# Three modulation sums moved to the tensor engine, a fourth final operand, earlier row gathers: one joined change to a two-layer trunk kernel

## The chip, the cores and the metric

The kernel runs on 1 NeuronCore of one Trainium2 chip as a single launch. The metric is device time in microseconds of that core. All data is float32; 512 tokens of width 1024 pass through two layers. "PE" is the tensor engine, "DVE" the vector engine, "ACT" the scalar engine, "POOL" GpSimd, "SP" the sync engine, which only issues transfers here.

## The reference, cut to what matters

```python
c_act = jax.nn.silu(c)
for layer in range(2):
    mod = c_act @ ada_w[layer] + ada_b[layer]              # (1024) @ (1024, 6144), 25 MB of weights a layer
    shift1, scale1, gate1, shift2, scale2, gate2 = jnp.split(mod, 6, axis=-1)
    h = rmsnorm(x, norm1_w[layer]) * (1 + scale1) + shift1
    if layer == 0:   # one projection -> pooling channels | q | k | v, pooling mixer and chunk attention, output projection
        mix = concat(pool_mixer(u), chunk_attention(q, k, v, rel_bias)) @ mix_w_out
    else:            # Mamba-2 mixer: projection, convolution, dt = softplus(h @ w_dt + dt_bias), chunked scan, gated norm
        mix = mamba2_mixer(h, ...)
    x = x + gate1 * mix
    h2 = rmsnorm(x, norm2_w[layer]) * (1 + scale2) + shift2
    x = x + gate2 * hier_moe(h2, ...)                        # 32 experts, top 2 inside the best group
return rmsnorm(x, final_norm_w)
```

## The kernel before, in words

**Modulation.** A third of a layer's `mod` (2048 columns) is a "part": `ada(layer, part, eng)` is a generator that loads eight 1 MB tiles of `ada_w` (128 rows by 2048 columns) into a ring of five buffers (tag `w8`) and, one step at a time, adds tile k times `ccol[:, k]` to the running sum on DVE (lines 189 and 191). After the eighth step four matrix products with a 128x32 block of ones add up the 128 partitions (line 198), each product writing its own 32 partitions of one PSUM bank. `ada(0, 1)`, `ada(0, 2)` and `ada(1, 0)` run inside the attention of layer 0, their steps spread over the calls of `fill()` by the list `FILL`; `ada(1, 1)` and `ada(1, 2)` run inside the Mamba mixer. Part 0 of layer 0, which the first norm needs, has its own code: `ada_loads` and `ada_sums(b)` (lines 507 to 580), in two halves b of four column blocks of 128 each for shift and scale.

**Start of layer 0.** `x` is loaded and transposed (line 532). `ada_sums(0)`, `modulate(0)`, `v_products(0)`, then the same for half 1: v = h @ w_v, with h and the weights each split into a high part (ACT, line 110) and a low part (DVE or POOL by the table `LO`, line 111), three products per pair (lines 434 to 436). `late_loads` (line 271) loads a row of zeros and three small vectors of layer 1 (`ssm_D`, `ssm_dt_bias`, `ssm_A_log`), each spread over 128 partitions by the transfer itself. Then `Dense` streams the columns of q, k and u: it loads (line 402), splits, and multiplies (lines 426 to 429). `scores(m)` (line 655) is the first step of attention.

**The order of the work.** The program fixes what depends on what, and a planner with estimated costs sets the order on each engine; each engine then runs its own list strictly in order, so that an instruction that waits holds up all behind it. Inside `manual_schedule` blocks the order is as written. Transfers issued by SP share one queue.

**The expert stage.** `Moe.run` loops over 17 units u of 128 token slots (16 pairs of experts and one overflow unit). In iteration u the PE does the hidden layer of unit u (line 1036), then the results of unit u-1 (line 1057). The results of most units are written to `yd` in DRAM (line 1067); at the end `ygather` (line 1176) adds the rows of `yd` to `x` with eight indirect transfers of 512 KB, two for each of the four token tiles. The units 8, 10, 13, 14, 15 and 16 do not go through DRAM: their results stay in SBUF as an "operand" (`parts_y`: high part, low part, one-hot matrix) and are added to `x` by products with the one-hot matrix (`products`, line 1079) and `padd` (line 1086). Units 8, 10 and 13 get this two iterations later; 14, 15 and 16 together in `combine`, after the loop. `combine` runs a list of steps (`STEPS` in layer 0): `xn` adds tile n, `hn` is a stage of the next norm of tile n, `wn` splits a weight of the next mixer. Before `combine`, `ahead()` loads the dt weight `wdt` (1024 rows of 32 columns), and splits it on ACT and DVE (lines 1438 to 1440).

Of the kernel before, what the change touches and what calls it, by code (L numbers as in the profile page):

```python
# [20 lines left out]
P = 128  # L21
T = 512
# [14 lines left out]
GAT = 15  # L37
# [16 lines left out]
HOLD = 7  # L54
PINS = 3
# [7 lines left out]
LO = {"v": "G", "e": "VVG", "m": "V", "o": "GVV", "s": "VV"}  # L63
# [4 lines left out]
STEPS = "x0 h0 x1 h1 h0 x2 h2 h0 h1 x3 h2 h3 h3 h0 h1 h2 h1 w1 h3 w2 h3 h2"  # L68
# [7 lines left out]
def trunk_kernel(ctx, tc, x, c, ada_w, ada_b, norm1_w, norm2_w, mix_w_in, pool_w, pool_scale,  # L76
# [86 lines left out]

    def ada(layer, part, eng, first=None):
# [19 lines left out]
        load(1)  # L184
        for k in range(KD):
# [8 lines left out]
        for _ in range(SLACK):  # L194
            yield
        p = ps(name=f"pada{layer}{part}")
        for q in range(4):
            PE.matmul(p[32 * q:32 * q + 32, :], ones[:, 0:32], ws[KD - 1][:, q * 512:(q + 1) * 512], start=True,
                      stop=True, skip_group_check=True)
# [290 lines left out]
    def even_mixer(layer):  # L490
        with ExitStack() as es:
# [15 lines left out]
            def ada_loads(b):  # L507
                SP.dma_start(adb[0:64:32, b * 512:(b + 1) * 512], dap(ada_b, b * 512, [[D, 2], [1, 512]]))
                for k in range(0, KD, 2):
# [3 lines left out]
                    aw[b, k], aw[b, k + 1] = (t[:, d].rearrange("p q n -> p (q n)") for d in range(2))  # L513
# [27 lines left out]
            def modulate(b):  # L541
# [12 lines left out]
            def v_products(b):  # L554
                for kk in (4 * b, 4 * b + 2):
# [8 lines left out]
            def ada_sums(b):  # L564
                V.tensor_scalar(aw[b, 0], aw[b, 0], ccol[:, 0:1], None, op0=ALU.mult)
                for k in range(1, KD):
                    V.scalar_tensor_tensor(aw[b, k], aw[b, k], ccol[:, k:k + 1], aw[b, k - 1], op0=ALU.mult,
                                           op1=ALU.add)
                p = ps(name=f"pada00{b}")
                for q in range(2):  # L570
                    PE.matmul(p[32 * q:32 * q + 32, :], ones[:, 0:32], aw[b, KD - 1][:, q * 512:(q + 1) * 512],
                              start=True, stop=True, skip_group_check=True)
                m = adb[0:64, b * 512:(b + 1) * 512]
                V.tensor_add(m, p[0:64], m)
                p = ps((P, 4, 64), name=f"pm00{b}")
                for q in range(4):
                    PE.transpose(p[:, q, :], m[:, q * P:(q + 1) * P], ident[0:64, 0:64])
                ks = slice(4 * b, 4 * b + 4)
                V.scalar_tensor_tensor(ab[:, 0, 0, ks], p[:, :, 32], 1.0, n1w[0][:, ks], op0=ALU.add, op1=ALU.mult)
                V.tensor_copy(ab[:, 0, 1, ks], p[:, :, 0])  # L580
# [3 lines left out]
            late_loads()  # L584
# [5 lines left out]
            v_products(1)  # L590
# [117 lines left out]
            adas = [ada(0, 1, V), ada(0, 2, V), ada(1, 0, V)]  # L708
# [81 lines left out]
    class Moe:  # L790
# [282 lines left out]
        def products(self, i, parts):  # L1073

            ps2 = [ps(name=f"pyc{self.layer}{i}{hf}") for hf in range(2)]
            for hf, p in enumerate(ps2):
                for n, part in enumerate(parts):
                    for q in range(2):
                        PE.matmul(p, part[2][:, i * P:(i + 1) * P], part[hf][:, q * 512:(q + 1) * 512],  # L1079
                                  start=n + q == 0, stop=n == len(parts) - 1 and q == 1)  # L1080
            return ps2
# [6 lines left out]
        def run(self, before_end=None):  # L1088
# [30 lines left out]
            def results(u, between=None):  # L1119
# [3 lines left out]
                             self.parts_y[max(u - NPAIR + 2, 0)] if last(u) else None)  # L1123

            ts = {}
            for u in range(NPAIR + 1):
# [20 lines left out]
                if 1 < u < NPAIR and last(u - 2):  # L1147
                    for i in range(NT):
                        self.padd(i, self.products(i, self.parts_y[:1]))
# [8 lines left out]
                if u == GAT:  # L1158
                    self.ygather()
                    for n in range(2):  # L1160
                        t = we([P, 2, 2 * T], F32R, f"yl{n}_{layer}")
                        o = we([P, 2, 2 * T], F32R, f"yo_{layer}")[:, 0, 0:T] if n else ot[:, T:2 * T]
                        self.parts_y.append((t[:, 0], t[:, 1], o))
                if u == 1:
# [256 lines left out]
    def odd_mixer(layer, prev):  # L1421
        with ExitStack() as es:
# [382 lines left out]
```

## Time and profile before

| what | value |
|---|---|
| median of three runs | 1119.99 us (1119.96 to 1123.87) |
| profiled execution: its own time, and its span | 1120.03 us, 1118.3 us |
| PE busy | 973.2 us, 87% of the span |
| DVE busy | 800.3 us, 72% |
| ACT, POOL busy | 388.9 us, 300.2 us |
| mean granted PE clock | 0.932 of full speed |
| moved by DMA | 263.88 MB, 236 GB/s |

The profile is of one execution. A matmul's duration overlaps that of the next, so the distance between the starts is its price where they follow without a gap. The granted clock has two levels, 1.2 and 2.4 GHz; a mean between 0.5 and 1.0 is a mixture. The stages in the trace: 0 to 86 us start of layer 0 (norm, v, first q and k), to 221 attention and pooling, to 262 output projection, to 301 router, to 435 experts, to 470 norm and dt of layer 1, to 862 Mamba mixer, to 930 its output projection, to 985 router, to about 1097 experts, then the last sums and the final norm.

### The profile page before, as it was taken

The numbers are of one execution on the slowest core, as the hardware profiler recorded it, in microseconds if no ns is written. First come the engines' busy times: TensorE is split into PE (matmuls) and PEld (weight loads), VectorE is DVE, ScalarE is ACT, GpSimd is POOL, SyncE is SP. The second block draws the span as 40 slices with busy tenths as digits, with TensorE's granted clock in tenths as the row PEclk, the third lists the DMA queues.
The fourth block names the chain that finished last, engine by engine and source line by source line (L and its number), as shares of the span: only waits on it lengthen the run. The fifth ranks groups of instructions, "written<-read, shape, count | busy, mean of one in ns | idle before, by whom it ended". The sixth has DMA issues, their size and how long they took to land. (4 is left out here: it accounts for less than half of the span.)

```text
span 1118.3 us, 15578 instructions
## 1 busy us (share of the span) xinstructions
PE 973.2 (87%) x5474; PEld 729.5 (65%) x5474; DVE 800.3 (72%) x1650; ACT 388.9 (35%) x753; POOL 300.2 (27%) x329
## 2 busy tenths in 40 slices
PE   4588788699699996898999899899989999799994
PEld 3466466388556654776786777777766878556653
DVE  6717986654565874789997989887797555564976
ACT  3135332425123232433444333443433325222332
POOL 4413100204231122411513416244142004231124
PEclk9789888799799998899999999999999999799997
DMA  9476876598699979536473465554334945699987
GB/s 332 139 265 168 286 282 252 215 364 330 209 364 414 411 229 255 210 107 198 143 264 88 135 194 159 190 158 113 126 109 152 333 154 209 204 390 415 412 278 185
DMA packets 140200, 263.88 MB, mean 236 GB/s; under 512 B 19917, under 2 KB 82337, under 8 KB 134994
## 3 DMA queue, kind: packets, MB, share of 16 engines
q1 hardware_dynamic: 129122, 235.40, 60.1%
q0 software_dynamic: 8928, 20.97, 7.2%
q10 hardware_dynamic: 2064, 6.42, 1.4%
q8 instruction: 47, 0.77, 0.3%
q14 instruction: 39, 0.32, 0.1%
HBM read 254.19 MB, written 20.11 MB: 245 GB/s over the span
## 5 line engine op out<-in xcount | busy, mean ns | idle before, releaser
L1036 PE MATMUL ph<-w,xT 128*64 128x256 f32 (+1 forms) x1152 | 132.1, 374 | 0.9 <-DVE xT L1020 0.7
L1036 PEld LDWEIGHTS ph<-w,xT 128*64 128x64 f32 x1152 | 86.8, 139 | 51.8 <-issue 10.9
L189 DVE SCALAR_TENSOR_TENSOR ada<-ada,ccol,ada 128x2048 f32<-128x2048 f32 x35 | 87.1, 2489 | 0.2
L1003 POOL DMA_INDIRECT xg<-xnd,toks x32 | 32.3, 1008 | 149.8 <-PE pxt L1015 122.6
L1057 PE MATMUL pyy<-w,hidT 128*64 128x512 f32 x272 | 65.9, 605 | 4.2 <-ACT hidT L1049 4.2
L1038 ACT ACTIVATE th<-ph 128x128 f32<-128x128 f32 x34 | 9.4, 278 | 160.8 <-PE pht L1047 137.1
L1022 ACT ACTIVATE xT<-pxt,mc 128x128 f32<-128x128 f32 x136 | 51.3, 458 | 17.9 <-PE pxt L1015 10.9
L1062 DVE SCALAR_TENSOR_TENSOR y<-pyy,wsl,gate 128x512 f32<-128x512 f32 x68 | 48.1, 744 | 6.1 <-DMA yd<-y 4.5
L1015 PE MATMUL pxt<-ident,xg 128*128 128x128 f32 x272 | 37.9, 284 | 15.5 <-DVEq L1383 7.9
L1086 DVE TENSOR_TENSOR x<-x,pyc 128x512 f32<-128x512 f32 x64 | 40.4, 682 | 14.1 <-PE pyc L1079 8.0
L1039 DVE SCALAR_TENSOR_TENSOR th<-th,ph 128x128 f32<-128x128 f32 x34 | 9.8, 287 | 55.7 <-ACT th L1038 55.7
L1020 DVE TENSOR_SCALAR xT<-pxt,mc 128x128 f32<-128x128 f32 x136 | 46.6, 405 | 1.4 <-PE pxt L1015 1.4
L1581 DVE TENSOR_SCALAR ms<-lb,acs 128x128 f32<-128x128 f32 x128 | 41.0, 359 | 5.9 <-DMA lb<-acd 3.6
L1015 PEld LDWEIGHTS pxt<-ident,xg 128*128 128x128 f32 x272 | 34.5, 194 | 16.2 <-issue 15.6
L1548 DVE SCALAR_TENSOR_TENSOR cvx<-pdx,cw,cvx 128x511 f32<-128x511 f32 (+2 forms) x48 | 35.4, 738 | 6.7 <-ACT cvx L1545 6.6
L1178 POOL DMA_INDIRECT x<-yd,row x16 | 25.1, 1571 | 50.0 <-DMA xgfw<-in_final_norm_w_dram 22.3
L1584 POOL TENSOR_TENSOR ms<-ms,cbm 128x512 f32<-128x512 f32 x16 | 32.0, 2001 | 17.8 <-ACT ms L1583 16.0
L1057 PEld LDWEIGHTS pyy<-w,hidT 128*64 128x64 f32 x272 | 16.5, 136 | 28.1 <-issue 19.4
L1079 PE MATMUL pyc<-yh,yot 128*128 128x512 f32 x128 | 33.7, 398 | 1.0 <-DVE yot L1070 1.0
L469 DVE TENSOR_TENSOR sor<-sor,gate 128x1024 f32<-128x1024 f32 x16 | 20.4, 1276 | 18.0 <-DMA sor<-in_ssm_w_out_dram 17.9
L661 ACT ACTIVATE scs<-scs,mx 128x512 f32<-128x512 f32 (+3 forms) x32 | 17.7, 555 | 36.2 <-DVE mx L660 32.8
L1079 PEld LDWEIGHTS pyc<-yh,yot 128*128 128x128 f32 x128 | 23.4, 188 | 9.6 <-issue 1.9
(1074 smaller groups left out, 2778.4 us busy)
## 6 DMA issues: line engine op xcount, KB each, us to landing
w<-in_moe_w_dram SPq DMA_DIRECT2D x192, 512.0 KB
ada<-in_ada_w_dram SPq DMA_DIRECT2D x40, 1024.0 KB
yd<-y SPq DMA_DIRECT2D x22, 512.0 KB
ada<-in_ada_w_dram SPq DMA_DIRECT2D x16, 512.0 KB
wx<-in_ssm_w_in_dram SPq DMA_DIRECT2D x16, 512.0 KB
wz<-in_ssm_w_in_dram SPq DMA_DIRECT2D x16, 512.0 KB
lb<-acd SPq DMA_DIRECT2D x32, 256.0 KB
sor<-in_ssm_w_out_dram SPq DMA_DIRECT2D x16, 512.0 KB
```

The costliest lines, as they stand in the source:

```text
L189: a = eng.scalar_tensor_tensor(ws[k], ws[k], ccol[:, k:k + 1], ws[k - 1], op0=ALU.mult, op1=ALU.add)
L1003: d = GP.indirect_dma_start(out=xg, out_offset=None, in_=xnd[:, :], in_offset=bass.IndirectOffsetOnAxis(ap=idx, axis=0), bounds_check=T - ...
L1015: PE.transpose(p[:, q, :], xv[:, 4 * hf + q, :], ident)
L1020: V.tensor_scalar(xT[:, k, :], p[:, q, :], a, b, op0=ALU.mult, op1=ALU.add)
L1022: S.activation(xT[:, k, :], p[:, q, :], AF.Identity, bias=b, scale=a)
L1036: PE.matmul(ph[64 * j:64 * j + 64, n:n + h, :], xT[:, k, 64 * j:64 * j + 64], w13[n][:, :, k, :], start=k == 0, stop=k == KD - 1, skip_gro ...
L1057: PE.matmul(py[64 * j:64 * j + 64], hT[:, 64 * j:64 * j + 64], w2[:, s], start=True, stop=True, skip_group_check=True)
L1062: V.scalar_tensor_tensor(y[:, s], py, self.wsl[:, slot:slot + 1], self.gate2[:, s], op0=ALU.mult, op1=ALU.mult)
L1079: PE.matmul(p, part[2][:, i * P:(i + 1) * P], part[hf][:, q * 512:(q + 1) * 512], start=n + q == 0, stop=n == len(parts) - 1 and q == 1)
L1086: V.tensor_add(xst["x"][i][:, s], xst["x"][i][:, s], p)
L1548: V.scalar_tensor_tensor(a[:, sh:], p[:, :T - sh], cw[:, tap, ch:ch + 1], a[:, sh:], op0=ALU.mult, op1=ALU.add)
L1581: V.tensor_scalar(ms[:, h, :], lb[:, h, :], acs[:, cq, 4 * g + h:4 * g + h + 1], 0.0, op0=ALU.subtract, op1=ALU.min)
```

## The change

The parts 0, 1 and 2 of layer 0's modulation and part 0 of layer 1 are summed on the PE: tile k is the moving operand of a product whose stationary operand is column k of `ccol`, broadcast to 32 columns, and the eight products accumulate in PSUM. `ada(..., None)` has one yield fewer. In `ada_sums` the even and odd k go to separate quarters of the bank, which are added after the transposes. The split's low parts in the v stage go to DVE alone, and `v_products` is called in finer pieces. `late_loads` loads the three vectors as one-partition rows; `head_rows` spreads them with a product with ones and three kinds of copies. In the experts, unit 13 is no longer added in iteration 15: it is a fourth operand of `combine`, whose tiles 0 and 1 are begun with three operands; `ygather` is issued at the end of iteration 14. The load of `wdt` moves to iteration 10, its split to a step `w0` of `combine`, its low part to POOL.

```diff
-GAT = 15
+GAT = 14
+EARLY = 10
-LO = {"v": "G", ...}
+LO = {"v": "V", ...}
-STEPS = "x0 h0 x1 h1 h0 x2 h2 h0 h1 x3 h2 h3 h3 h0 h1 h2 h1 w1 h3 w2 h3 h2"
+STEPS = "x0 h0 x1 h1 h0 x2 h2 h0 h1 x3 h2 h3 h3 h0 h1 h2 h1 w0 w1 h3 w2 h3 h2"
...
+    def ada_mm(p, k, w, first, last):
+        for q in range(4):
+            PE.matmul(p[32 * q:32 * q + 32, :], ccol[:, k:k + 1].to_broadcast([P, 32]), w[:, q * 512:(q + 1) * 512],
+                      start=first, stop=last, skip_group_check=True)
...
             yield
+            if not eng:
+                if not k:
+                    p = ps(name=f"pada{layer}{part}")
+                ada_mm(p, k, ws.pop(k), k == 0, k == KD - 1)
+                continue
...
     def late_loads():
         SP.dma_start(yd[len(MAIN) * P:, :], zrow)
+        hrow = st_.tile([1, 3, 32], F32, name="hrow")
+        for n, src in enumerate((ssm_D, ssm_dt_bias, ssm_A_log)):
+            SP.dma_start(hrow[:, n, :], dap(src, 0, [[0, 1], [1, 32]]))
+        return hrow
+
+    def head_rows(hrow):
+        p = ps((P, 3, 32), name="phr")
+        PE.matmul(p, ones[0:1, :], hrow, start=True, stop=True)
         for q in range(2):
-            SP.dma_start(dcol[64 * q:64 * q + 64, :], dap(ssm_D, q, [[0, 64], [2, 16]]))
-        SP.dma_start(dtb, dap(ssm_dt_bias, 0, [[0, P], [1, 32]]))
-        SP.dma_start(arow, dap(ssm_A_log, 0, [[0, P], [1, 32]]))
+            V.tensor_copy(dcol[64 * q:64 * q + 64, :], p[64 * q:64 * q + 64, 0, q::2])
+        V.tensor_copy(dtb, p[:, 1, :])
+        V.tensor_copy(arow, p[:, 2, :])
...
-                    (V if g % 2 else GP).tensor_sub(parts[1][g], xa[g], parts[0][g].bitcast(F32))
+                    V.tensor_sub(parts[1][g], xa[g], parts[0][g].bitcast(F32))
...
             def ada_sums(b):
-                V.tensor_scalar(aw[b, 0], aw[b, 0], ccol[:, 0:1], None, op0=ALU.mult)
-                for k in range(1, KD):
-                    V.scalar_tensor_tensor(aw[b, k], aw[b, k], ccol[:, k:k + 1], aw[b, k - 1], op0=ALU.mult,
-                                           op1=ALU.add)
                 p = ps(name=f"pada00{b}")
+                for k in range(0, KD, 2):
+                    for d in range(2):
+                        for q in range(2):
+                            o = 64 * d + 32 * q
+                            PE.matmul(p[o:o + 32, :], ccol[:, k + d:k + d + 1].to_broadcast([P, 32]), aw[b, k][:, d, q],
+                                      start=k == 0, stop=k == KD - 2, skip_group_check=True)
...
             modulate(1)
-            v_products(1)
+            v_products(2)
+            head_rows(hrow)
+            v_products(4, 6)
...
-            adas = [ada(0, 1, V), ada(0, 2, V), ada(1, 0, V)]
+            adas = [ada(0, 1, None), ada(0, 2, None), ada(1, 0, None)]
...
-                if 1 < u < NPAIR and last(u - 2):
+                if 1 < u < NPAIR - 1 and last(u - 2):
...
                 if u == GAT:
                     self.ygather()
-                    for n in range(2):
-                        t = we([P, 2, 2 * T], F32R, f"yl{n}_{layer}")
-                        o = we([P, 2, 2 * T], F32R, f"yo_{layer}")[:, 0, 0:T] if n else ot[:, T:2 * T]
+                    wide = [wp.tile([P, 2048], F32R, tag="w8", name=f"y{n}_{layer}", bufs=W8) for n in ("l0", "oh")]
+                    y = [wide[0].rearrange("p (h n) -> p h n", h=2)]
+                    y += [we([P, 2, 2 * T], F32R, f"yl{n}_{layer}") for n in (1, 2)]
+                    for t, o in zip(y, (ot[:, T:2 * T], wide[1][:, 0:T], wide[1][:, T:2 * T])):
                         self.parts_y.append((t[:, 0], t[:, 1], o))
...
-                p = [self.products(i, self.parts_y) for i in range(NT)]
+                p = self.products((0, 1), self.parts_y[:-1], False)
+                p = self.products((0, 1), self.parts_y[-1:], True, p)
+                p += self.products((2, 3), self.parts_y, True)
...
-                w = prev.y_tile("wdt")
-                wdt.append(w[:, 0:256].rearrange("p (k c) -> p k c", k=KD))
+            def early():
+                wdt.append(small.tile([P, KD, NLOG], F32, tag="wr", name="wdt", bufs=1)[:, :, 0:32])
                 SP.dma_start(wdt[0], w_in[:, 6144:6176].rearrange("(k p) c -> p k c", p=P))
+            def splits(n):
+                if n:
+                    return dense.split(n, GP)
                 wdt.append(ws4(F32R, "whl")[:, 0:512].rearrange("p (k c) -> p k c", k=KD))
-                split(wdt[1][:, :, 0:32], wdt[1][:, :, 32:64], wdt[0], V)
+                split(wdt[1][:, :, 0:32], wdt[1][:, :, 32:64], wdt[0], GP)
```

## Rows read from the trace of the kernel before

**Rows 1.** From the table by stage: from and to in us, its length, busy time (and instructions) of PE, PE weight loads, DVE, ACT and POOL, granted PE clock, DMA share, GB/s.

```profile
34.00:58.00 24.00, 15.35 (x56) 10.95 (x56) 13.91 (x13) 2.49 (x3) 9.50 (x4) 0.78 0.30 84
...
85.70:221.00 135.30, 108.25 (x500) 76.38 (x500) 108.71 (x222) 52.33 (x127) 23.44 (x20) 0.86 0.69 241
...
301.00:403.00 102.00, 100.92 (x762) 62.38 (x762) 66.49 (x189) 31.24 (x92) 19.61 (x19) 1.00 1.01 392
...
435.00:470.00 35.00, 22.64 (x138) 21.19 (x139) 23.94 (x50) 15.75 (x33) 15.65 (x17) 0.76 0.74 270
470.00:862.00 392.00, 361.07 (x1826) 287.50 (x1825) 337.85 (x530) 151.65 (x219) 127.46 (x90) 0.97 0.49 150
...
1082.00:1118.30 36.30, 20.41 (x104) 12.40 (x99) 24.19 (x53) 10.90 (x27) 18.40 (x17) 0.84 0.77 174
```

**Rows 2.** From the DMA queues between 36 and 60 us: mean busy share in 40 equal slices (tenths), packets and how many of them are small.

```profile
DMA  9610000000000000000011001111112677879996
...
DMA packets 5080, 1.74 MB, mean 73 GB/s; under 512 B 2434, under 2 KB 4906, under 8 KB 5069
```

**Rows 3.** From the instructions in order of time, those that issue transfers: start, duration of the issue.

```profile
30.99 3.52 SPq L274 DMA_DIRECT2D dcol<-in_ssm_D_dram  x2
...
41.09 4.32 SPq L402 DMA_DIRECT2D wq<-in_mix_w_in_dram  x1
```

**Rows 4.** From the waits between 30 and 62 us: which engine and line waited for whom, us in total, times, longest.

```profile
ACT q0h L110 <- DMA wq<-in_mix_w_in_dram: 13.0, 1, 13.0
...
PE pdq L426 <- ACT q0h L110: 7.4, 1, 7.4
...
PE accv L436 <- POOL hlo L550: 2.2, 1, 2.2
```

**Rows 5.** From the instructions in order of time on PE and ACT in the start stage: start, duration, in brackets the idle time before them.

```profile
11.60 8.78 PE L532 MATMUL pt<-dgx,x 128*128 128x128 f32 x64
25.26 1.92 PE L571 MATMUL pada<-ada,ones 128*32 128x512 f32 x4 [4.88 <-DVE ada L567]
...
37.80 0.80 PE L436 MATMUL accv<-vw0h,hlo 128*128 128x512 f32 x1 [2.16 <-POOL hlo L550]
...
42.13 0.39 PE L434 MATMUL accv<-vw0h,hhi 128*128 128x512 f32 x1
...
43.05 0.39 PE L435 MATMUL accv<-vw0l,hhi 128*128 128x512 f32 x1
...
85.73 0.70 PE L655 MATMUL sc<-kT,qT 64*128 64x512 f32 x2 [0.69 <-ACT kT L696]
...
23.13 1.06 ACT L110 ACTIVATE vw0h<-vr 128x1024 fp32r<-128x1024 f32 x1 [2.33 <-DMA vr<-in_mix_w_in_dram]
```

**Rows 6.** From the list of groups of DVE instructions between 85.7 and 221 us: count, busy time and mean ns of one, idle time before them.

```profile
L189 DVE SCALAR_TENSOR_TENSOR ada<-ada,ccol,ada 128x2048 f32<-128x2048 f32 x21 | 52.2, 2485 | 0.2
```

**Rows 7.** From the waits of PE between 85 and 222 us.

```profile
PE pada L198 <- DVE ada L189: 9.1, 1, 9.1
PE sc L655 <- DVE c L111: 6.7, 1, 6.7
PE pdu L426 <- DVE mx L658: 3.9, 2, 2.0
PE pdq L426 <- DVE mx L658: 3.4, 1, 3.4
```

**Rows 8.** From the instructions in order of time on PE: the four products with ones of `ada(0, 1)` and of `ada(0, 2)` (eight instructions each).

```profile
128.85 1.93 PE L198 MATMUL pada<-ada,ones 128*32 128x512 f32 x8
...
164.16 1.06 PE L198 MATMUL pada<-ada,ones 128*32 128x512 f32 x8
```

**Rows 9.** From the instructions in order of time from 405 to 448 us, on PE, ACT, DVE and POOL.

```profile
407.02 3.94 PE L1079 MATMUL pyc<-yh,yot 128*128 128x512 f32 x16
...
422.74 0.72 PE L1079 MATMUL pyc<-yh,yot 128*128 128x512 f32 x2
...
433.92 0.61 PE L1079 MATMUL pyc<-yl,yo 128*128 128x512 f32 x2
...
440.78 3.78 PE L350 MATMUL pt<-xh,x 128*128 128x128 f32 x16 [6.25 <-DVE xh L347]
446.87 1.38 PE L350 MATMUL pt<-xh,x 128*128 128x128 f32 x10 [2.31 <-DVE xh L347]
...
435.05 0.42 ACT L110 ACTIVATE whl<-wdt 128x256 fp32r<-128x256 f32 x1 [10.75 <-DMA wdt<-in_ssm_w_in_dram]
...
435.84 2.47 DVE L1086 TENSOR_TENSOR x<-x,pyc 128x512 f32<-128x512 f32 x4
...
409.34 1.60 POOL L1178 DMA_INDIRECT x<-yd,row  x1 [19.25 <-DVE x L1086]
```

**Rows 10.** From the DMA queues between 416 and 436 us, the line of the queue that SP issues to (packets, MB, share of 16 engines).

```profile
q1 hardware_dynamic: 1057, 0.14, 5.6%
```

**Rows 11.** From the instructions in order of time at the end: SP's write of unit 12's rows, POOL's first gather, DVE's sums for unit 13 and the first sum of the end.

```profile
1070.17 0.33 SPq L1067 DMA_DIRECT2D yd<-y  x1
...
1081.47 1.60 POOL L1178 DMA_INDIRECT x<-yd,row  x1 [22.31 <-DMA xgfw<-in_final_norm_w_dram]
...
1076.86 3.68 DVE L1086 TENSOR_TENSOR x<-x,pyc 128x512 f32<-128x512 f32 x6 [1.91 <-PE pyc L1079]
...
1098.70 1.28 DVE L1086 TENSOR_TENSOR x<-x,pyc 128x512 f32<-128x512 f32 x2 [4.06 <-DMA x<-yd,row]
```

More of the change, by code (lines that the diff above doesn't have):

```diff
@@ L184, in ada @@
         load(1)
+        p = None
         for k in range(KD):
@@ L193, in ada @@
                 tc.keep_in_program_order(a)
-        for _ in range(SLACK):
+        for _ in range(SLACK if eng else 0):
             yield
[L196 to L199, printed above, removed]
+        if eng:
+            p = ps(name=f"pada{layer}{part}")
+            for q in range(4):
+                PE.matmul(p[32 * q:32 * q + 32, :], ones[:, 0:32], ws[KD - 1][:, q * 512:(q + 1) * 512], start=True,
+                          stop=True, skip_group_check=True)
         m = b
@@ L512, in ada_loads @@
                         SP.dma_start(t[:, d], dap(ada_w, (k + d) * P * 6 * D + b * 512, [[6 * D, P], [D, 2], [1, 512]]))
-                    aw[b, k], aw[b, k + 1] = (t[:, d].rearrange("p q n -> p (q n)") for d in range(2))
+                    aw[b, k] = t
             def v_loads(b):
@@ L564, in ada_sums @@
             def ada_sums(b):
-                V.tensor_scalar(aw[b, 0], aw[b, 0], ccol[:, 0:1], None, op0=ALU.mult)
-                for k in range(1, KD):
-                    V.scalar_tensor_tensor(aw[b, k], aw[b, k], ccol[:, k:k + 1], aw[b, k - 1], op0=ALU.mult,
-                                           op1=ALU.add)
                 p = ps(name=f"pada00{b}")
[L570 to L575, printed above, removed]
+                for k in range(0, KD, 2):
[4 more added lines that the diff above has]
+                                      start=k == 0, stop=k == KD - 2, skip_group_check=True)
+                m = adb[:, b * 512:(b + 1) * 512]
+                V.tensor_add(m, p, m)
+                p = ps((P, 4, P), name=f"pm00{b}")
                 for q in range(4):
-                    PE.transpose(p[:, q, :], m[:, q * P:(q + 1) * P], ident[0:64, 0:64])
+                    PE.transpose(p[:, q, :], m[:, q * P:(q + 1) * P], ident)
                 ks = slice(4 * b, 4 * b + 4)
-                V.scalar_tensor_tensor(ab[:, 0, 0, ks], p[:, :, 32], 1.0, n1w[0][:, ks], op0=ALU.add, op1=ALU.mult)
-                V.tensor_copy(ab[:, 0, 1, ks], p[:, :, 0])
+                two = st_.tile([P, 2, 4], F32, name=f"two{b}")
+                V.tensor_copy(two, p[:, :, 0:64:32].rearrange("p q n -> p n q"))
+                V.tensor_add(two, two, p[:, :, 64:P:32].rearrange("p q n -> p n q"))
+                V.scalar_tensor_tensor(ab[:, 0, 0, ks], two[:, 1], 1.0, n1w[0][:, ks], op0=ALU.add, op1=ALU.mult)
+                V.tensor_copy(ab[:, 0, 1, ks], two[:, 0])
             ada_loads(1)
             v_loads(1)
-            late_loads()
+            hrow = late_loads()
             ada_sums(0)
@@ L1071, in results, with products @@
                                     op0=ALU.add, op1=ALU.is_equal)
[L1073 to L1081, printed above, removed]
+        def products(self, tiles, parts, stop=True, sums=None):
+            out = sums or [[ps(name=f"pyc{self.layer}{i}{hf}") for hf in range(2)] for i in tiles]
+            for i, ps2 in zip(tiles, out):
+                for hf, p in enumerate(ps2):
+                    for n, part in enumerate(parts):
+                        for q in range(2):
+                            PE.matmul(p, part[2][:, i * P:(i + 1) * P], part[hf][:, q * 512:(q + 1) * 512],
+                                      start=not sums and n + q == 0, stop=stop and n == len(parts) - 1 and q == 1,
+                                      skip_group_check=True)
+            return out
         def padd(self, i, ps2):
@@ L1086, in padd, with run @@
                 V.tensor_add(xst["x"][i][:, s], xst["x"][i][:, s], p)
-        def run(self, before_end=None):
+        def run(self, before_end=None, early=None):
             layer = self.layer
@@ L1451, in after @@
                     yield from hT_tile(layer, i, h_hi, h_lo)
-                prev.combine([after(i) for i in range(NT)], STEPS, lambda n: dense.split(n, GP))
+                prev.combine([after(i) for i in range(NT)], STEPS, splits)
                 prev.close()
```

14 lines of the change are left out of this document (8 added, 6 removed).

## The prediction

> **What bounds the kernel now.** I read the table by stage first, then the waits and the order of time inside the stages that the change touches. The table [rows 1] shows that no one engine sets the whole time. From 301 to 403 us (experts) PE is busy 100.9 of 102 us and DMA is full as well; from 470 to 862 us (Mamba mixer) DVE is busy 338 of 392 us beside PE at 361. The change leaves the work of these two almost as it is. Time is lost elsewhere: from 34 to 58 us, where PE works 15.4 of 24 us at a granted clock of 0.78 while DMA is busy 0.30 of the time; in attention (85.7 to 221 us), where PE and DVE each work 108 of 135 us and PE's clock is 0.86; from 435 to 470 us, with PE at 22.6 of 35 us and a clock of 0.76; and after 1082 us.
>
> In the first of these a small thing blocks a large one. SP issues the two loads of `dcol` at 31 us and the first weight of q at 41.1 us [rows 3]. The queue view shows DMA going from full to nearly idle soon after 36 us and staying there for some 15 us, with 2434 packets below 512 bytes [rows 2]; `dcol` by its shape is 2 x 64 x 16 single elements, 2048 of these. The weight of q stands behind them: ACT waits 13.0 us for it, with the modulation of half 1 behind that wait, and PE 7.4 us [rows 4].
>
> In attention, 23.1 of PE's 27.05 idle us end with a DVE instruction [rows 7], and 52.2 us of DVE's work are the running sums of modulation [rows 6]. At 435 us ACT has waited 10.75 us for the dt weight; DVE's first sum of `combine` follows at 435.84, and PE's first transpose of the new norm at 440.78, though PE's own products ended at 434.5 [rows 9]. At the end the first gather starts at 1081.47 and the first tile is added at 1098.70, the wait ended by that tile's gather [rows 11].
>
> **The change part by part.** Negative numbers are gains.
>
> *Start, -12.* Before, half 0's products with ones start at 25.26, and the v products run without a break from 37.80 [rows 5]: 12.5 us for those products, the row's sum, transposes, modulation and splits. After, the sums follow the transposes of x on PE, which end at 11.60 + 8.78 = 20.4; the weights are there, since the v weight queued behind them was being split at 23.13 [rows 5]. A step of one pair of k is eight instructions on four quarters, the form that took 1.06 us at the full and 1.93 us at half clock [rows 8]: four steps end at 20.4 + 4.2 = 24.6, or 28.1. The rest costs what it did, 37.8 - 25.3 - 1.9 = 10.6, less the 2.2 us for which PE waited for POOL's low part [rows 4], now DVE's: 33. Half 1's sums no longer stand on DVE among modulation and splits, for which I take one more: 32 instead of 37.8, -6. From there to the first scores before took 85.7 - 37.8 = 48 us. It holds 142 products of 0.23 us, the distance of the rows at 42.13 and 43.05 [rows 5], 32.7 us; after, 4 x 1.06 for half 1, 2 us for a slow beginning, 3 us for waits: 42, another -6. Between -4 (sums at half clock in both halves, +7, and some of the wait left) and -15 (no waits).
>
> The cover for the rest: the spreading of the three rows is one small product and four small copies on a DVE freed of sixteen sums; if it is late nobody asks for `dtb` before layer 1. What is late next is the supply of split weights, whose buffers come free only as products end.
>
> *Attention, -6.* Taken from DVE: three times seven sums, 52.2 us [rows 6], and the first steps. Added to PE: 24 steps of 1.06 = 25.4 us, less the three products with ones (1.93 and 1.06 are in the rows; 4.9 with the third at the larger): +20.5, so 128.8 us busy. PE's idle 27 us I cut to 9: the two waits for DVE's sums go (9.1 and 6.7), the others shrink but some stay, because PE still waits for the first scores to be read before it has a free bank, and one bank is now held through a whole part. The clock: a mean of 0.86 means the low level in 28% of the stage, 38 us; 11 to 30 us of these PE was busy, so 5 to 15 us were lost to it. With fewer holes I give back 9. Sum 128.8 + 9 - 9 = 129 against 135.3. Ends: 118 (idle 4, all 15 back), -17; and 144 (idle 15, none back), +8. Behind a PE step that waits for its tile stands all of PE's list, and behind SP's next tile of `ada_w`, which waits for a buffer, stand the next weights of q, k and u.
>
> Here a rule may be weighed against a row. Four products take 1.06 us [rows 8]. The Trainium skill, "FP8 and Floating Point Precision", section TensorE Precision Notes, states that true FP32 takes four passes through the array. Worked out by that page alone, as an estimate, a step of four products of 512 columns is 4 x 4 x 512 columns at 2.4 GHz, 3.4 us; 24 steps would be 82 instead of 25 us, and the whole change would come out near 1150. The row has four quarters sharing the time of one, in the form that the change uses; the sum goes by the row.
>
> *From layer 0 to layer 1, -8.* Unit 13's 16 products leave iteration 15 (3.94 us, row at 407.02) and come back at the end: 48 took 434.5 - 422.7 = 11.8 us, 0.245 each, so 3.9. PE's products end at 434.5 as before. The wait of ACT for the dt weight goes: its buffer was a result tile, now it is loaded at iteration 10. Tile 0 needs its second gather, the fifth; at the end of the kernel it was added 17.2 us after the first gather began [rows 11], which here is 409.34 + 17.2 = 426.6 [rows 9] even with no gain. So DVE's sums no longer hold PE: tile 0's transposes follow at 434.5 (440.78), at full clock 2.2 us instead of 3.78 (ten took 1.38), and tile 1's at 434.5 + 6.1 - 1.6 = 439 instead of 446.87 [rows 9]. Between -5 (slow clock, first step alone) and -10. The load's 1024 rows now fall where DMA is full: the 1057 packets of SP's queue were 5.6% of 20 us [rows 10], 1.1 us, which PE's lead hides, or not: +1. The low part on POOL is a quarter of a weight's; it stands between splits that come later anyway.
>
> *End, -1.* Gathers wait for the write of unit 12's rows, issued at 1070.17. The first gather began 3.3 us after tile 0's sums for unit 13 (1076.86, two of six in 3.68 us: 1078.1) [rows 11]. So what held it was a transfer, and without those sums it is still held; I take 1 us, 0 to 3.3. In layer 0 the sums did hold it.
>
> Sum: -12 - 6 - 8 - 1 = -27. The profiled execution took 1120.03 us (span 1118.3), as the median, 1119.99: 1093.
>
> **The rivals.** *PE takes the place of DVE:* attention gives nothing (idle 11, 2 us of clock back, 138) and the start -8: 1120 - 8 - 8 - 1 = 1103. For it: PE is already at 108 of 135 us; against: DVE's sums head the two longest waits.
>
> *More:* start -14, attention -15, transition -9, end -3: 1079. For it: every hole of PE in attention ends with DVE; against: scores, exponent and transposes form a chain of their own.
>
> *No change within 0.5%* (5.6 us, about what a measurement can tell from none): the mixer, where DVE is at 338 of 392 us, would have to wait out what comes earlier. No row shows it waiting for time.
>
> *Slower, one mechanism:* PE runs dry on `ada_w`. A tile of 1.05 MB at 392 GB/s [rows 1] takes 2.7 us, a step 1.06; with the ring empty each step waits 1.6 us, and PE, unlike DVE, has everything behind it. To lose the 27 us and 5.6 more, 33 us, 21 of 24 steps would have to find it empty: 1126 or more. Against: five buffers, and DMA at 0.69 in this stage.
>
> *Quarters one after the other:* if the four products of a step did not share their time, a step would be 4 x 1.06 = 4.2 us of PE, 24 of them 102 instead of 25 us: 1170. Against it: the 1.06 us are those of all four, in eight instructions [rows 8]. The Trainium skill's page named above, with its four passes and no sharing, gives the 1150 stated there.
>
> **How the numbers follow.** My forecast, 1093 (alone 1085 to 1101), gets 0.55; PE in DVE's place 0.22; more 0.13; no change 0.05; PE dry 0.03; quarters in a row 0.02. Faster by over 0.5% is 0.55 + 0.22 + 0.13 = 0.90, within it 0.05, slower 0.05. The range goes from just below the 1079 case to beyond 1103: 1077 to 1108; less than that leaves out too much, since start and attention each have ends some 10 us from my value.
>
> **What would show it.** Start: DMA busy around 40 us, q's weight split before 50, scores before 76. Attention: PE's idle below 15 us, clock above 0.9, DVE below 60 us; wrong if PE waits for transfers of `ada` or is busy above 135. Transition: PE's transposes directly behind `pyc`, no wait of ACT for the dt weight. End: first gather less than 2 us earlier relative to the write of unit 12. The prediction is wrong if the mixer or the experts, left alone, become longer by what the start gains, or if a step on PE takes more than 1.3 us.

## The result, and the profile after

The kernel after takes 1090.74 us (median of 4 runs, 1089.82 to 1094.89) against 1120.91 of the kernel before in the same comparison: ratio 0.9734, 95% interval 0.9702 to 0.9765. The forecast was 1093, in a range of 1077 to 1108. The profiled execution is the longest of the four, 1094.89 us with a span of 1093.0; it stands 25 us below the profiled execution of before, where the medians stand 30 apart.

The start stage first: from the table by stage, then in order of time on PE, DVE, SP and ACT.

```profile
31.80:77.10 45.30, 41.37 (x184) 30.21 (x184) 14.02 (x23) 14.78 (x18) 3.12 (x3) 0.93 0.68 230
36.00:46.00 10.00, 10.00 (x59) 5.86 (x58) 1.60 (x2) 2.12 (x2) 0.04 (x1) 0.89 0.18 67
```

```profile
22.09 3.64 PE L593 MATMUL pada<-ada,ccol 128*32 128x512 f32 x32
31.83 0.79 PE L457 MATMUL accv<-vw0h,hhi 128*128 128x512 f32 x1 [4.45 <-ACT hhi L572]
40.70 3.64 PE L593 MATMUL pada<-ada,ccol 128*32 128x512 f32 x32
45.01 1.21 DVE L112 TENSOR_TENSOR vw4l<-vr,vw4h 128x1024 fp32r<-128x1024 f32 x1
46.25 0.39 SPq L425 DMA_DIRECT2D wq<-in_mix_w_in_dram  x1
51.15 1.04 ACT L111 ACTIVATE q0h<-wq 128x1024 fp32r<-128x1024 f32 x1
75.50 1.06 ACT L111 ACTIVATE q1h<-wq 128x1024 fp32r<-128x1024 f32 x1 [2.80 <-DMA wq<-in_mix_w_in_dram]
76.46 0.58 ACT L723 ACTIVATE kT<-pdk 128x512 f32<-128x512 f32 x1
77.09 2.43 PE L682 MATMUL sc<-kT,qT 64*128 64x512 f32 x16 [2.73 <-ACT kT L723]
```

Four steps take 3.64 us, 0.91 each. The v products start at 31.83 (forecast 32) and the first scores at 77.09 instead of 85.73 [rows 5]. The issue of q's weight takes 0.39 instead of 4.32 us [rows 3], but it comes later, at 46.25, because its buffer is held by a split (`vw4l`, which ends at 46.22) that stands on DVE behind the second sum. DMA therefore still has a hole (0.18 from 36 to 46 us), of another kind: in it nothing is asked for. PE now works through it (10.0 of 10 us), which is why it costs less than the hole of before.

Attention by stage, PE's waits in it, and steps on PE:

```profile
77.10:201.10 124.00, 117.97 (x669) 73.49 (x669) 53.49 (x199) 50.90 (x125) 21.67 (x19) 1.00 0.76 270
```

```profile
PE pm L306 <- DVE adab L215: 3.1, 1, 3.1
PE sc L682 <- ACT kT L723: 2.7, 1, 2.7
PE py L664 <- DVE pl L659: 1.7, 1, 1.7
```

```profile
85.11 4.50 PE L168 MATMUL pada<-ada,ccol 128*32 128x512 f32 x40
97.15 1.06 PE L168 MATMUL pada<-ada,ccol 128*32 128x512 f32 x8
```

124 instead of 135.5 us, with PE idle for 6, its clock at 1.00, and DVE at 53.5 instead of 108.7 us. Five steps in a row take 4.50, so one is 0.9; a single one takes 1.06, as in [rows 8], and 12 of the 24 stand alone. None of PE's waits in this stage is for a tile of `ada_w`.

From layer 0 to layer 1, in order of time on PE, DVE and POOL:

```profile
388.44 1.60 POOL L1210 DMA_INDIRECT x<-yd,row  x1 [18.24 <-DVE th L1067]
399.13 0.73 PE L1107 MATMUL pyc<-yh,yot 128*128 128x512 f32 x2
406.71 1.28 DVE L1115 TENSOR_TENSOR x<-x,pyc 128x512 f32<-128x512 f32 x2 [5.29 <-PE pyc L1107]
413.77 1.95 PE L373 MATMUL pt<-xh,x 128*128 128x128 f32 x16
418.02 4.10 PE L373 MATMUL pt<-xh,x 128*128 128x128 f32 x32 [2.30 <-DVE xh L370]
427.47 0.33 PE L1512 MATMUL pdt<-sh_hi,whl 128*64 128x256 f32 x1 [1.66 <-POOL whl L112]
```

The transposes of the new norm follow the products with no idle time between (6.25 before, [rows 9]), at 1.95 instead of 3.78 us. DVE's first sum waits for PE, no longer for anything of the dt weight. A small new wait is there: the low part on POOL, which I had put at nothing, is waited for by `pdt` for 1.66 us.

The end, on SP, POOL, PE and DVE:

```profile
1044.98 0.33 SPq L1094 DMA_DIRECT2D yd<-y  x1
1055.90 1.68 POOL L1210 DMA_INDIRECT x<-yd,row  x1 [22.27 <-issue]
1062.55 0.73 PE L1107 MATMUL pyc<-yh,yot 128*128 128x512 f32 x2
1073.52 1.29 DVE L1115 TENSOR_TENSOR x<-x,pyc 128x512 f32<-128x512 f32 x2 [8.71 <-DMA x<-yd,row]
```

The first gather starts 10.9 us behind the write of unit 12's rows (11.3 before, [rows 11]), and from it to the end of the span are 37.1 us (36.8). PE and DVE are done earlier, and DVE's wait for the gather grows from 4.06 to 8.71 us.

### The profile page after: what moved, and what is told of

It reads as the page before. It is cut to its first block, busy times and chain, and to the rows that moved or that the text cites. A ratio compares the mean times of both kernels' runs of the same rounds, so it can differ in the third digit from the quotient of the medians.

```text
span 1093.0 us, 15960 instructions
## 1 busy us (share of the span) xinstructions
PE 985.5 (90%) x5700; PEld 726.6 (66%) x5700; DVE 715.6 (65%) x1607; ACT 388.7 (36%) x753; POOL 282.9 (26%) x324
## 5 line engine op out<-in xcount | busy, mean ns | idle before, releaser
L1066 DVE SCALAR_TENSOR_TENSOR th<-th,ph 128x128 f32<-128x128 f32 x34 | 9.8, 287 | 57.2 <-ACT th L1065 57.2
L1115 DVE TENSOR_TENSOR x<-x,pyc 128x512 f32<-128x512 f32 x48 | 30.4, 682 | 20.9 <-DMA x<-yd,row 11.4
L1620 DVE TENSOR_SCALAR ms<-lb,acs 128x128 f32<-128x128 f32 x128 | 37.8, 335 | 6.5 <-DMA lb<-acd 4.2
L202 DVE SCALAR_TENSOR_TENSOR ada<-ada,ccol,ada 128x2048 f32<-128x2048 f32 x14 | 34.9, 2496 | 0.1
L1670 PE MATMUL pyd<-ms,xdt 128*64 128x128 f32 x256 | 20.2, 291 | 9.5 <-DVE ms L1623 9.5
L1622 ACT ACTIVATE ms<-ms 128x512 f32<-128x512 f32 x32 | 19.8, 623 | 24.6 <-DVE ms L1620 24.5
L1637 PE MATMUL pxd<-ident,cvx 128*128 128x128 f32 x64 | 11.6, 316 | 17.2 <-DVE cvx L1591 17.2
(1079 smaller groups left out, 2770.2 us busy)
```

Of the source, the lines that this page charges most:

```text
L1115: V.tensor_add(xst["x"][i][:, s], xst["x"][i][:, s], p)
L1620: V.tensor_scalar(ms[:, h, :], lb[:, h, :], acs[:, cq, 4 * g + h:4 * g + h + 1], 0.0, op0=ALU.subtract, op1=ALU.min)
```

## The experiments

The change in parts, each put alone into the kernel before; then single costs and waits in the kernel after. The marks, in us, are read from each profile's order of time; "mixer" is from the first to the last row of `pxd`, "rest" from there to the end of the span. Each row of marks is one execution, so that a spread in them may be of kernels or of executions.

```
kernel       first    output   atten-  new norm  mixer  rest    ratio to before
             scores   proj.    tion    transp.                  (95% interval)
before        85.7    221.2    135.5    440.8    328.8  291.3
loads_only    80.1    215.6    135.4    435.1    329.2  290.8   0.9940 (0.9915-0.9965)
sums_only     81.2    211.7    130.5    432.5    332.0  291.4   0.9958 (0.9935-0.9981)
start_all     75.6    206.2    130.6    426.9    328.4  290.8   0.9900 (0.9870-0.9929)
att_only      86.4    214.2    127.8    434.1    331.3  292.8   0.9928 (0.9903-0.9952)
wdt_only      85.6    218.4    132.8    434.2    330.4  293.6   0.9947 (0.9922-0.9972)
moe_wdt       84.8    216.4    131.6    431.6    328.4  291.6   0.9938 (0.9911-0.9964)
after         77.1    201.1    124.0    413.8    331.4  291.6   0.9734 (0.9702-0.9765)
act_write     75.5    202.1    126.6    416.0    331.5  286.8   0.9711 (0.9668-0.9754)
v_third       74.7    203.5    128.8    416.4    331.0  291.6   0.9812 (0.9778-0.9847)
combo         73.5    203.6    130.2    416.7    325.4  289.3   0.9749 (0.9716-0.9782)
three_edits   73.0    194.3    121.3    410.2    332.2  287.5   0.9648 (0.9623-0.9673)
```

**The start.** Whole, its loads alone, its sums alone:

```diff
 loads_only: late_loads() and head_rows(hrow) of the kernel after; the rest as before
 sums_only:  ada_sums, v_products and LO["v"] of the kernel after; late_loads() as before
 start_all:  both
```

> The kernel before with the start stage of the kernel after, and nothing else of the change: the sums of half 0 and half 1 as products with c, the low parts on DVE, the three head rows as one short row each. Theory A (the three parts of the change add up, as the two traces suggest): first scores near 77 us instead of 85.7, all of it kept to the end, 9 us, ratio 0.992 (0.990 to 0.994). Theory B (the parts hang together: the attention stage is bound by DVE and would wait for its sums of modulation whatever the start does): first scores earlier, but 3 us or less at the end, ratio above 0.997.

> The kernel before with the short loads alone: ssm_D, ssm_dt_bias and ssm_A_log as three rows on one partition, spread by a product with ones, in place of loads of single elements and of broadcast rows. Theory A (the element loads hold up q's weight, and the sums on DVE are a second, separate cost): q's weight split before 45 us instead of 56, first scores 4 to 6 us earlier, ratio 0.995 to 0.996. Theory C (the jam is the whole gain of the start): as much as the whole start stage, 8 to 9 us, ratio 0.992. Theory D (DVE's sums are the whole gain, the weight is waited for only because DVE is late): under 1 us, ratio above 0.999.

> The kernel before with the sums of half 0 and half 1 in the start as products with c and the low parts on DVE, while dcol, dt_bias and A_log are loaded as before, element by element. With the whole start stage the first scores came at 75.6 us, with the short loads alone at 80.1, before at 85.7. Theory A (two costs one after the other): 4 to 5 us, first scores near 81 us, ratio 0.996. Theory J (the late weight of q covers what the sums give, so that they only count once it is there): q's weight split at 54 us or later as before, first scores at 84 us or later, under 2 us, ratio above 0.998.

First scores 10.1, 5.6 and 4.5 us earlier: the two costs add up at this mark, and theory A holds for all three. Its detail did not: the expectation for `loads_only` names 56 us for the split of q's weight before, where the trace has 58.99, and asks for less than 45 after. With the short loads q's weight is issued at the same time as before (41.09, [rows 3]) but split at 50.79 instead of 58.99, held at the end by a buffer and not by the transfer:

```profile
41.46 0.39 SPq L411 DMA_DIRECT2D wq<-in_mix_w_in_dram  x1
50.79 1.06 ACT L110 ACTIVATE q0h<-wq 128x1024 fp32r<-128x1024 f32 x1 [4.38 <-PE accv L444]
```

With the sums alone (ACT, in order of time) the weight is as late as before, yet the gain is there: the modulation of half 1 now stands ahead of the wait for it, so that wait has less behind it.

```profile
48.80 1.99 ACT L549 ACTIVATE hhi<-xa 128x1024 fp32r<-128x1024 f32 x2
59.41 1.06 ACT L110 ACTIVATE q0h<-wq 128x1024 fp32r<-128x1024 f32 x1 [8.62 <-DMA wq<-in_mix_w_in_dram]
```

**Attention alone**, `adas` and `ada` of the kernel after in the kernel before:

```diff
-            adas = [ada(0, 1, V), ada(0, 2, V), ada(1, 0, V)]
+            adas = [ada(0, 1, None), ada(0, 2, None), ada(1, 0, None)]
```

> The kernel before with the three parts of modulation in attention as products with c on PE, and nothing else of the change. Theory A (in attention PE and DVE waited for each other, and the work that moved costs PE 24 steps of 0.9 us): from the first scores to the first product of the output projection 124 us instead of 135.5, PE's clock at 1.00 there, ratio 0.989 to 0.991 (10 to 12 us). Theory B (PE takes DVE's place, and the stage is shorter in the kernel after only because the start left its weights loaded earlier): 132 us or more, ratio above 0.997.

```profile
86.40:214.20 127.80, 119.68 (x668) 74.62 (x669) 58.01 (x200) 52.40 (x127) 21.84 (x20) 0.99 0.75 261
```

Theory A in kind (B asked for 132 us and more), at 0.9928 less than it asked for: 8 us, not 10 to 12. The table suggests why. Kernels with DVE's sums took 130.5 to 135.5 us here with the same code in this stage, mean 132.8 of six; those with all steps on PE took 124.0 to 127.8, mean 126.1 of three. The profiles of the kernels before and after happen to be the ends of both: 11.5 us between them, 6.7 between the means.

**What a step costs where it stands**, and whether four quarters share their time:

```diff
 few_steps, in ada(): one step of eight
-                ada_mm(p, k, ws.pop(k), k == 0, k == KD - 1)
+                if not k:
+                    ada_mm(p, k, ws[k], True, True)
 one_wide, in ada_mm(): one product for the four quarters
+        PE.matmul(p, ccol[:, k:k + 1].to_broadcast([P, P]), w[:, 0:512], start=first, stop=last, ...)
```

> The kernel after, with one step of products per part of modulation in attention instead of eight: 21 of 24 steps are left out, and with them seven eighths of those three sums; the weights are still loaded. It prices the steps where they stand. Theory A (the stage is bound by PE, and the steps cost what they take): 21 x 0.9 = 19 us less, 105 us from the first scores to the output projection. Theory F (the steps fill holes that the chain of scores, exponent and transposes leaves on PE, and so keep its clock up): the holes come back and the granted clock falls below 0.95, 115 us or more, so that a step of 0.9 us costs under half of that.

> The kernel after, with one product of 128 equal columns per step in place of four quarters of 32 columns each, in the three parts of modulation in attention: three quarters of the weight's columns are left out of the sums. Theory A (the four quarters share the time of one product): a step still takes 0.9 us, and the stage 124 us. Theory G (quarters follow one another, and 0.9 us is the sum of four): a step takes 0.23 us, 24 of them 16 us less, the stage 110 us or less.

```profile
75.60:175.10 99.50, 95.97 (x500) 69.65 (x501) 52.36 (x197) 49.52 (x124) 21.35 (x19) 1.00 0.89 331
```

```profile
84.17 4.45 PE L167 MATMUL pada<-ada,ccol 128*128 128x512 f32 x10
```

Without 21 of the 24 steps the stage takes 99.5 us, 24.5 less, and the clock stays at 1.00: theory F falls, and A undershoots. PE's busy time falls by 22.0, its idle time by 2.5 us. So PE bounds the stage after the change. By these two profiles a step costs 1.17 us there, 1.05 of them busy time, which is not less than it takes. The second row is five steps of one wide product each, in `one_wide`: 4.45 us, where five steps of four quarters took 4.50; the whole stage took 123.3 us, as theory A has it, and theory G asked for 110 or less. One reading is left open by this: a product could take the longer the more stationary columns it has, so that four quarters in a row would also come to one wide product. The rows of before speak against it: at half clock two quarters took 1.92 us (four instructions, [rows 5]) and four quarters 1.93 (eight instructions, [rows 8]). The quarters share their time.

**One part back on DVE**, since DVE now works under half of the stage:

```diff
-            adas = [ada(0, 1, None), ada(0, 2, None), ada(1, 0, None)]
+            adas = [ada(0, 1, None), ada(0, 2, None), ada(1, 0, V)]
```

> The kernel after, with the last of attention's three parts of modulation, that of layer 1, back on DVE; nothing is left out. Leaving out 21 of the 24 steps shortened the stage by 24 us, more than the 19 us that they take, so PE bounds it, while DVE is busy 53 of its 124 us. Theory A (a balance between the two pays): PE loses 8 steps of 0.9 and gains one product with ones, 6 us less, minus 1 to 2 us of waits for sums of 2.5 us each among the scores' work on DVE: 4 to 5 us, ratio to before 0.969. Theory K (each sum on DVE holds up the chain of scores, and PE waits for it as in the kernel before): no gain or a loss, 0.973 or above.

```profile
PE pada L212 <- DVE ada L202: 8.6, 1, 8.6
```

```profile
74.70:203.50 128.80, 114.82 (x611) 75.25 (x612) 69.30 (x206) 50.95 (x125) 22.92 (x20) 0.93 0.76 260
```

Theory K: 0.9812, 9 us worse than the kernel after. In the stage PE loses 3.2 us of work and gets back the very wait that headed [rows 7], now 8.6 us, and with it a clock of 0.93. Seven sums in a chain end when DVE finds time for them, and PE stands before the product that needs the last. The stage is 4.8 us longer than in the profile after; where the rest of the 9 went, the profile, which is of the shortest of its four runs, doesn't show. `combo`, with the same part on DVE, has the wait again, 11.1 us there.

**The transition**: the dt weight alone, then with the fourth final operand and the earlier gathers.

```diff
 wdt_only: EARLY, early(), splits() and "w0" in STEPS of the kernel after
 moe_wdt:  these, GAT = 14, products(), parts_y and combine() of the kernel after
```

> The kernel before with the dt weight alone moved (loaded in iteration 10 into a buffer of its own, its split at a step of its own with the low part on POOL); the final operands and the gathers stay as they were. Theory A (ACT's wait for that weight is what held the first sums and so the transposes by 6 us): the transposes of the new norm follow pyc directly or with under 1 us between, and the gain is 5 to 6 us of the 6 to 7 that the layer steps gave together, ratio 0.995. Theory I (without the earlier gathers the second gather of tile 0 or DVE's sums for unit 13 hold it anyway): under 2 us, ratio above 0.998.

> The kernel before with the fourth final operand, the gathers issued in iteration 14 and the dt weight moved, in both layers, and nothing of start and attention. Theory A: PE's transposes of the new norm follow pyc directly, 6 to 7 us earlier relative to the end of the products, and the end of the kernel gives 0.4 us, since the first gather stays 11 us behind the write of unit 12's rows: 7 to 8 us, ratio 0.993 to 0.994. Theory E (the mixer gives part of it back: its span was 2.6 us longer in the profile of the kernel after): 4 to 5 us, ratio 0.996.

```profile
433.70 0.62 PE L1080 MATMUL pyc<-yl,yo 128*128 128x512 f32 x2
434.17 1.95 PE L351 MATMUL pt<-xh,x 128*128 128x128 f32 x16
```

The dt weight by itself puts the transposes directly behind the products (rows of `wdt_only`) and gives 0.9947, nearly all of the 0.9938 of both: theory A; I and E fall. What the fourth operand adds cannot be told from nothing. The mixer, which I feared would give something back, took 325.4 to 332.2 us over the table with no visible relation to what was changed; its 2.6 us in the profile after lie inside that spread and are not shown to be an effect of the change.

**The end**: the writes of units 11 and 12 on another queue.

```diff
-                             self.parts_y[max(u - NPAIR + 3, 0)] if last(u) else None)
+                             self.parts_y[max(u - NPAIR + 3, 0)] if last(u) else None, S if u >= GAT - 3 else SP)
```

> The kernel after, with the writes of the rows of units 11 and 12 issued on ACT's queue instead of SP's, where they stand behind the last expert weights; nothing is left out. Theory A (the write is late because it stands in one queue with the weights, 11 us from its issue to the first gather): the first gather comes within 5 us of the issue, and as DVE waited 8.7 us for the gathers at the end, the end gives 5 to 6 us; ratio to before 0.968 (against 0.973 for the kernel after), the transition as it is. Theory H (the transfer itself takes its 10 us, as DMA is full of weights whatever the queue): first gather 10 us or more behind the issue, no gain, 0.973.

```profile
1042.65 0.33 ACTq L1094 DMA_DIRECT2D yd<-y  x1
1050.17 1.60 POOL L1210 DMA_INDIRECT x<-yd,row  x1 [15.69 <-DMA w<-in_moe_w_dram]
1063.42 0.73 PE L1107 MATMUL pyc<-yh,yot 128*128 128x512 f32 x2
1069.64 1.28 DVE L1115 TENSOR_TENSOR x<-x,pyc 128x512 f32<-128x512 f32 x2 [3.96 <-PE pyc L1107]
```

Between the theories: the gather comes 7.5 us behind the write, neither 5 nor 10. That is enough for DVE's first sum to wait for PE's product again; from the first of the last products to the end of the span are 26.1 us instead of 30.5. The whole kernel's interval overlaps that of the kernel after, so the 4.4 us are seen in the profile alone.

The wait on SP has a second half that theory A did not count: the write is issued late. DVE and SP in the kernel after, then DVE, SP, POOL and PE in `one_wide`, whose end is the same code:

```profile
1040.16 1.40 DVE L1089 SCALAR_TENSOR_TENSOR y<-pyy,wsl,gate 128x512 f32<-128x512 f32 x2
1043.71 0.33 SPq L1006 DMA_DIRECT2D w<-in_moe_w_dram  x1
1044.98 0.33 SPq L1094 DMA_DIRECT2D yd<-y  x1
```

```profile
1036.10 0.33 SPq L1004 DMA_DIRECT2D w<-in_moe_w_dram  x1
1037.84 1.40 DVE L1087 SCALAR_TENSOR_TENSOR y<-pyy,wsl,gate 128x512 f32<-128x512 f32 x2
1039.26 0.33 SPq L1092 DMA_DIRECT2D yd<-y  x1
1048.80 1.60 POOL L1208 DMA_INDIRECT x<-yd,row  x1 [17.49 <-issue]
1060.23 0.74 PE L1105 MATMUL pyc<-yh,yot 128*128 128x512 f32 x2
```

In the kernel after the rows are ready at 1041.56, and the write follows 3.4 us later, behind the last load of a weight. In `one_wide` that load was issued before the rows were ready; the write follows at once, the gather 9.5 us behind it, and from the first of the last products to the end are 25.7 us, though the write is on SP. `few_steps` is alike, with 9.8 and 26.1 us. So the edit takes away a wait that the same code does not have in every execution; why SP was ahead in these two is not known, and what the edit is worth by itself stays open.

**Together.** `combo` has this write, kT copied by DVE and the part on DVE; `three_edits` leaves that part on PE and moves its transposes behind the next product instead.

```diff
-                S.activation(kT, pk, AF.Copy)
+                V.tensor_copy(kT, pk)
 three_edits, in ada():
         if part == 0:
+            if not eng:
+                yield
             mod_cols(layer, m)
```

> The kernel after with three edits: the writes of units 11 and 12 on ACT's queue, the last of attention's three parts of modulation on DVE, and kT copied by DVE instead of ACT, where that copy stood behind a split which waits for a transfer; nothing is left out. Theory A (they add up): 3 to 5 us from the end, 4 to 5 from attention, 2 from the first scores, together 9 to 12 us below the kernel after, 1079 to 1082 us, ratio 0.963 to 0.965. Rival K (attention does not gain, and the write on another queue only shortens a wait that the next one takes over): 1088 us or more, ratio 0.971 or above.

> The kernel after with three edits, each for one wait that its traces show, and all sums on PE; nothing is left out. The writes of units 11 and 12 go on ACT's queue (from the last products to the end 26.1 us where that was tried, 30.5 in the kernel after); kT is copied by DVE (PE waited 2.7 us for ACT before the first scores); the transposes of the last part of modulation in attention stand one product behind its sum (PE waited 3.1 us for DVE). Theory A (the three waits end last where they stand, so what they took is gained): 4 + 2 + 3 us, 1080 to 1085 us, ratio to before 0.963 to 0.968. Rival L (other waits take over, as with the sums put back on DVE): 1088 us or more, ratio 0.970 or above.

`combo` is no better than the kernel after, as rival K had it: its attention (130.2 us) gives back what its start and end gain. `three_edits` is better, as its theory A had it: median 1083.79 us of 6 runs, ratio 0.9648, with an interval that lies wholly below that of the kernel after. It is the fastest version here, and each of the three waits is gone or replaced by a shorter one: first scores at 73.0 with PE's wait for kT at 0.9 us, attention 121.3 us, the write's gather 7.5 us behind it. What each of the three gives by itself was not measured. Attention by stage, and PE's wait before the first scores:

```profile
73.00:194.30 121.30, 118.22 (x667) 73.56 (x668) 53.73 (x200) 48.72 (x121) 20.84 (x20) 1.00 0.78 277
PE sc L684 <- DVE kT L725: 0.9, 1, 0.9
```

## Why the prediction was right, point by point

**Start, -12.** In the four kernels of the table that have the whole start stage and kT on ACT the first scores come at 74.7 to 77.1 us, mean 75.7, against 85.6 in the four without any of it: -9.9. The first half of the step held: v products at 32 forecast, 30.2 to 31.8 measured. Its terms were each off and cancel: in the profile after the sums began 1.7 us later than put (22.09 for 20.4), took 0.6 less, and from their end to the products it was 1.3 shorter. The second was mis-sized: from there to the scores I had 42 us, and the profile after has 45.3. I gave 2 us for a slow beginning, where the products run at 0.43 instead of 0.23 us each until 38 us, 14 of them, 2.8 us; and 3 for waits, where 3.9 were idle, 2.7 of them for kT, which stands on ACT behind a split that waits for a transfer. The rest of the 3.3 us I have not traced. So "scores before 76" fails in the profile after by 1 us, and "split before 50" by 1.15; "DMA busy around 40 us" fails outright, at 0.18 from 36 to 46 us.

**Attention, -6.** Right in the mean (6.7) and by the kernel that has it alone (8), by terms that were each off. The sum was 128.8 busy + 9 idle - 9 of clock; the profile after has 118.0 busy, at full clock, and 6 idle. The price of a step held: 1.06 in the sum, 1.05 of busy time by `few_steps`. The clock was worth more than the 9 us. In the profile before PE was busy for 25 us in the four stretches at the low level:

```profile
123.90:134.10 10.20, 5.97 (x16) 2.77 (x17) 9.15 (x25) 3.30 (x8) 0.65 (x2) 0.50 0.78 267
154.60:161.40 6.80, 5.76 (x14) 4.50 (x15) 6.79 (x23) 2.23 (x6) 0.00 (x0) 0.50 0.96 368
168.30:175.10 6.80, 5.50 (x17) 4.26 (x16) 2.44 (x12) 2.29 (x8) 0.52 (x1) 0.50 0.42 145
202.40:216.10 13.70, 7.78 (x30) 4.93 (x31) 6.80 (x13) 3.26 (x9) 4.45 (x4) 0.50 0.86 324
```

Half of that, 12.5 us, is an estimate of what the low level cost. Two of the products with ones that the sum takes off stand in these stretches, so that 1.7 us (twice 1.93 - 1.06) are counted in both; 128.8 - 12.5 + 1.7 comes to the 118.0 measured. Idle was put 3 us too high. The signs in the profile (idle below 15, clock above 0.9, DVE below 60) all held.

**Transition, -8.** By its mean over the table (output projection to the transposes, 220.1 us in the five kernels without any of it, 214.0 in the six with all of it) 6.1 us, and from there to the first `pxd` 57.2 against 55.6: 7.7. The cause given held: the dt weight. Putting the split's low part on POOL was not free, 1.66 us.

**End, -1.** Zero, the lower bound given. The reason was the right one: the gather is held by a transfer, the write, and DVE's work ahead of it does not matter. That the write is also issued late, behind the last weights on SP's queue, was not in the prediction.

**Sum.** By the marks 9.9 + 6.7 + 7.7 + 0 = 24 us, three less than forecast; by the medians 30, three more. By the ratios the parts alone give 1.00 + 0.72 + 0.62 = 2.34%, the whole 2.66%; as each of these is known to 0.25 or 0.3 either way, the parts neither help nor hinder each other as far as this can tell, and the difference stays open. That 1093 came within 3 us of 1090.74 is in part luck, as the marks and the medians lie on either side of it.

**The rivals.** PE does become attention's bound, as the first rival had it, but without its price: the stage is shorter by what PE had waited for DVE and by what the low clock had cost. (That rival's own 138 us for attention are 3 us more than the nothing that its sum counts; by them it would be 1106, not 1103.) "More" was wrong in every stage by the marks, and its total, 1079, lies 12 us from the 1090.74. "No change" asked the mixer to wait out what comes earlier; its length showed no relation to that. PE did not run dry on `ada_w`: no wait for it stands in attention. A step of quarters one after the other, 4.2 us, was not seen.

The estimate of 3.4 us a step, from the Trainium skill's "FP8 and Floating Point Precision", section TensorE Precision Notes, is refuted for a step and borne out for a product: one f32 product of 512 columns, four passes by that page, would be 4 x 512 / 2.4 GHz = 0.85 us as an estimate, and `one_wide` has 0.89. What I had not joined to it is the Trainium skill's "TensorEngine Tiling (Array Packing)", section Key Properties, by which different tiles can run their products in parallel; the 4.50 against 4.45 us agree.

## What to carry to other kernels

Work that two engines hand back and forth is worth moving to the one that is "busier", if the hand-over is what both wait for: here PE took 24 steps more and the stage became shorter; handing a third back to an engine that was idle more than half the time made it longer again. Before a stage's gain is read from two profiles, look at how much that stage varies between profiles that have the same code in it (attention 5 us, mixer 7 us, the end 5 us here). A tiny load can cost what stands behind it in its queue, and a small write or copy is late by what stands ahead of it: look at the queue, and move the small one out of it.

## What the runs showed of the hardware

Four f32 products on four quarters of 32 columns took the time of one product of 128 columns, 0.90 against 0.89 us a step; at half clock two quarters took 1.92 us and four 1.93.

A write of 0.5 MB on SP's queue was followed by the gather that needs it 9.5 to 11.4 us after its issue in eleven profiles, and in nine of them it was issued 3.1 to 4.1 us after its rows were ready, behind loads of weights; on ACT's queue it was issued at once and followed in 7.2 to 7.5 us, with a DMA share in that time of 1.02 in `act_write` and 0.77 in the kernel after. By the Trainium skill's "DMA: Bandwidth & Descriptors", section Queues, rings and completion order, each DMA engine takes packets in turn from the queues that have work; the shorter time agrees with it, though no run here shows the order of the packets.
